# A hybrid attention layer with an MLP: the down weights of the MLP split in two by converting and adding DMAs, up and down weights in separate rings

## The chip, the cores and the metric

The kernel is one program on one core of a Trainium2 chip. The metric is device microseconds of one execution. The kernel before takes 668.31 us, the median of three runs (668.25 to 668.99).

## The reference

One decoder layer for 512 tokens of width 1024, in float32. What matters here:

```python
h = h + hybrid_mixer(rmsnorm(h, g_attn), ...)      # attention: 8 FoX heads, 8 NSA heads, one output projection
h = h + squared_relu_mlp(rmsnorm(h, g_mlp), w_up, w_down)
return rmsnorm(h, g_final)

def squared_relu_mlp(h, w_up, w_down):             # w_up 1024 x 4096, w_down 4096 x 1024
    return jnp.square(jax.nn.relu(h @ w_up)) @ w_down
```

## The kernel before

**Two halves for every operand.** TensorE reads operands rounded to a shorter float ("fp32r" in the profile). To keep float32's precision each operand is held as a rounded high part and a rounded low part (value minus high part), and each product is three matmuls into the same bank: high by high, low by high, high by low (`mm3`, lines 190 to 192). All weights lie in DRAM as one tensor `wp` of numbered pieces, each 128 partitions by 1024 (512 KB); `next_piece` counts them up, so pieces are used in a fixed order.

**Rings.** A `Ring` turns a piece into its two parts: SP loads it into a raw buffer (L139), ScalarE copies it, rounded, into the high part (L164), and a subtraction, on VectorE nearly always, gives the low part (L118). The first ring, `ring`, lies in a pool at the right end of SBUF, cuts each piece into two halves of 512 columns, and holds three pieces and two raws. When attention's first buffers are closed, a second ring, `ring2`, opens at the left end of SBUF (L1098 to L1101); it takes whole pieces, 1024 wide, and holds six and three raws. In the MLP, `mlp_piece` (L1103) takes a piece from `ring` where its number modulo 9 is below 3, and from `ring2` else. So both kinds of weights come from both rings.

**The MLP** (L1127 and on) has 8 steps. In the first half of a step, four "up" units: each multiplies one up piece with the activations `uh` and `ul` (24 matmuls of 512 columns into one bank), and ScalarE, GpSimd and VectorE turn the bank into one of four columns of `ah` and `al`: ReLU into `mt` (L1139), its square rounded into `ah` (L1140), the same square in full on GpSimd into `ma` (L1141), and `ma` less `ah` into `al` (L1142). In the second half, "down": four down pieces times `ah` and `al`, for four blocks of 128 tokens (4 times 24 matmuls), with the sums added to the residual by VectorE (L1156). The first three up units are begun inside attention's output projection, with pieces 38 to 40 from `ring`. `uh` and `ul` lie at the right end of SBUF; `ah`, `al`, `mt` and `ma` lie in the pool `mp` at the left end. In the profile's names a matmul `O<-uh,wh` belongs to an up unit (weights held in the array, activations moving), and `O<-wh,ah` to down (activations held, weights moving).

**What sets the order.** TensorE's order is the order of the code (`manual_schedule`, L75). VectorE, ScalarE, GpSimd and SP are under a second such block through the attention (L77 to L1037), so that its instructions keep the code's order among themselves; what the code has behind it a scheduler places, and it can put such an instruction between those of the attention where its buffers allow it. Each engine then runs its own list strictly in order, and so do the queues of the engines that issue DMAs.

**The end of attention**, where the MLP's first weights are prepared. Around 264 to 290 us the last attention heads are finished while NSA's half of the output projection fills TensorE. GpSimd normalises the scores `sp` (L726) and sums squares `sq` (L783). ScalarE copies the transposed scores out of the banks (`pth`, L748), copies head outputs (`ot`, L766) and scales them (`yTf`, L779); VectorE makes the low parts (`ptl` L118, `yTf` L784) and evacuates the projection's only bank "acc" into `xr` (L895), which TensorE needs empty before it begins the next unit.

Of the kernel before, what the change touches and what calls it, by code (L numbers as in the profile page):

```python
# [11 lines left out]
F32R = mybir.dt.float32r  # L12
AF = mybir.ActivationFunctionType
ALU = mybir.AluOpType

P = 128
# [37 lines left out]
def hybrid_layer(tc, x, xT, wp, wfg, cst, gfin, out):  # L54
    nc = tc.nc
    uid = [0]

    def nm(s):
        uid[0] += 1
        return f"{s}_{uid[0]}"  # L60

    def f32(ap):
        return ap.bitcast(F32)
# [3 lines left out]
    def open_pool(name, side, **kw):  # L67
        stacks[name] = ExitStack()
        return stacks[name].enter_context(tc.tile_pool(name=name, bufs=1, side=side, reuse_waits="tile", **kw))
# [37 lines left out]
    def w2k(n, dt=F32):  # L107
        return atp.tile([P, S], dt, tag="w2", name=nm(n), bufs=4)
# [4 lines left out]
    def bank(tag):  # L113
        return psp.tile([P, 512], F32, tag=tag, name=nm(tag), bufs=n_banks[tag])
# [5 lines left out]
    next_piece = [0]  # L120
# [61 lines left out]
    ring = Ring(rp, 3, 2, 2)  # L182

    def part(w, a, n):

        k, c = divmod(a, 1024 // len(w[0]))
        return w[0][k][:, c:c + n], w[1][k][:, c:c + n]

    def mm3(ps, lh, ll, rh, rl, first, last):
        nc.tensor.matmul(ps, lh, rh, start=first, stop=False)  # L190
        nc.tensor.matmul(ps, ll, rh, start=False, stop=False)  # L191
        nc.tensor.matmul(ps, lh, rl, start=False, stop=last)  # L192
# [19 lines left out]
    ps = bank("acc")  # L212
# [301 lines left out]
    w = ring.piece()  # L514
    natural_piece(q_banks, w, 3, (0,))
    ps = bank("acc")
# [34 lines left out]
    ps = bank("acc")  # L551
# [6 lines left out]
    ps = bank("T")  # L558
# [11 lines left out]
    t = w2k("f2c")  # L570
# [12 lines left out]
    for m in range(4):  # L583
        w = ring.piece()
# [44 lines left out]
    w = ring.piece()  # L629
# [3 lines left out]
    w = ring.piece()  # L633
# [240 lines left out]
    def tokens(tb):  # L874
        return slice(tb * P, tb * P + P)
# [194 lines left out]
    def up_mm(ps, w, kts):  # L1070
        for kt in kts:
            mm3(ps, *part(w, kt * P, P), uh[:, kt, :], ul[:, kt, :], kt == 0, kt == 7)
# [4 lines left out]
    for tb in range(NT):  # L1077
        ps = bank("OOSS"[tb])
# [10 lines left out]
    for i, t in enumerate(("acc", "S", "O")):  # L1089
        w = ring.piece()  # L1090
        ps = bank(t)
# [6 lines left out]

    r2p = open_pool("ring2", "left")
    mp = open_pool("mp", "left")  # L1100
    ring2 = Ring(r2p, 6, 3, 1)  # L1101

    def mlp_piece():  # L1103
        return (ring if next_piece[0] % 9 < 3 else ring2).piece()

    ssum = cp.tile([P, NT], F32, name="ssum")
    nc.vector.tensor_tensor(ssum, ssh[:, :, 0], ssh[:, :, 1], op=ALU.add)
# [8 lines left out]
    def scalar(n):  # L1116
        return cp.tile([P, 1], F32, tag="sc" + n, name=nm(n), bufs=2)
# [5 lines left out]
    def nbank():  # L1123
        un[0] += 1
        return bank(tags[un[0] % 8])

    for e in range(8):  # L1127
        ah = mp.tile([P, 4, S], F32R, tag="ah", name=nm("ah"), bufs=2)
        al = mp.tile([P, 4, S], F32R, tag="al", name=nm("al"), bufs=2)
        for f in range(4):  # L1130
            if early:
                w, ps = early.pop(0)
                up_mm(ps, w, range(4, NK))
            else:
                w, ps = mlp_piece(), nbank()
                up_mm(ps, w, range(NK))
            t = mp.tile([P, S], F32, tag="mt", name=nm("mt"), bufs=2)
            a = mp.tile([P, S], F32, tag="ma", name=nm("ma"), bufs=2)
            nc.scalar.activation(t, ps, AF.Relu)  # L1139
            nc.scalar.activation(ah[:, f, :], t, AF.Square)  # L1140
            nc.gpsimd.tensor_tensor(a, t, t, op=ALU.mult)  # L1141
            nc.vector.tensor_sub(al[:, f, :], a, f32(ah[:, f, :]))  # L1142
        wd = [mlp_piece() for _ in range(4)]
        for tb in range(NT):
            groups = [(0, 512), (512, 256), (768, 256)] if (e, tb) == (7, NT - 1) else [(0, 512), (512, 512)]
            pss = [nbank()[:, 0:n] for _, n in groups]
            tok = tokens(tb)
            for fs in ((0, 1, 2), (3,)) if tb == 0 else ((0, 1, 2, 3),):
                for ps, (c, n) in zip(pss, groups):
                    for f in fs:  # L1150
                        mm3(ps, ah[:, f, tok], al[:, f, tok], *part(wd[f], c, n), f == 0, f == 3)
            last = groups[-1]
            ob = mp.tile([P, D], F32, tag="ob", name=nm("ob"), bufs=2) if e == 7 else None
            for i, (ps, (c, n)) in enumerate(zip(pss, groups)):
                h = h1[:, tb, c:c + n]
                nc.vector.scalar_tensor_tensor(h, ps, r2s[:, tb:tb + 1], h, op0=ALU.mult, op1=ALU.add)  # L1156
                if e == 7:
                    (nc.gpsimd if i == 0 else nc.vector).tensor_tensor(ob[:, c:c + n], h, gfb[:, c:c + n], op=ALU.mult)
                    jo = mp.tile([P, S], F32, tag="mt", name=nm("jo"), bufs=2)
                    ss = sso[:, tb, i:i + 1]  # L1160
                    nc.scalar.activation(jo[:, 0:n], h, AF.Square, accum_out=ss)
                    if i == 0:
                        eb = scalar("eb")
                        nc.vector.tensor_scalar(eb, ss, 1.0 / D, EPS, op0=ALU.mult, op1=ALU.add)
                    elif i < len(groups) - 1:
                        nc.vector.scalar_tensor_tensor(eb, ss, 1.0 / D, eb, op0=ALU.mult, op1=ALU.add)
            if e == 7:
                v, t, r = scalar("v"), scalar("t"), scalar("r")
                nc.scalar.activation(t, ss, AF.Ln, scale=1.0 / D, bias=eb)
                nc.scalar.activation(r, t, AF.Exp, scale=-0.5)  # L1170
                nc.vector.scalar_tensor_tensor(v, ss, 1.0 / D, eb, op0=ALU.mult, op1=ALU.add)
                nc.vector.scalar_tensor_tensor(t, r, v, r, op0=ALU.mult, op1=ALU.mult)
                nc.vector.tensor_scalar(t, t, -0.5, 1.5, op0=ALU.mult, op1=ALU.add)
                for half in range(2):
                    cols = slice(512 * half, 512 * half + 512)
                    nc.vector.tensor_scalar(ob[:, cols], ob[:, cols], r, t, op0=ALU.mult, op1=ALU.mult)
                    nc.sync.dma_start(out[tokens(tb), cols], ob[:, cols])
# [103 lines left out]
```

## Time and profile before

| what | value |
|---|---|
| median of 3 runs | 668.31 us |
| the profiled execution's own time | 669.01 us |
| its span in the trace | 667.2 us |
| TensorE busy | 650.7 us, 98% of the span |
| VectorE, ScalarE, GpSimd busy | 405.6, 312.8, 170.6 us |
| TensorE's granted clock | full speed throughout |
| the chain that ended last | TensorE 86%, VectorE 8%, the rest 6% |
| DRAM read, mean rate | 59.81 MB, 93 GB/s over the span |

The span is the time from the first to the last instruction that the trace shows; 1.8 us of the execution lie around it. The share of TensorE says that nothing else bounds the kernel for long, and the chain agrees; the other engines have room on the whole. Between about 262 and 654 us, which holds the end of attention, the output projection and all of the MLP, TensorE shows no idle time of note.

### The profile page before, as it was taken

Reading aid. Unit: us, or ns where it says so; the run is one execution under the profiler, and the core shown is the slowest. Engines: PE = TensorE matmul, PEld = TensorE weight load, DVE = VectorE, ACT = ScalarE, POOL = GpSimd, SP = SyncE. Lnnn points to the kernel's source line nnn. Section 1 sums busy time; section 2 is a strip of 40 time slices with the busy share of each in tenths; the row PEclk is TensorE's granted clock in tenths of the full one; section 3 lists DMA queues with packets and bytes.
Section 4 is the critical chain, followed back from the end, with each engine's and each line's share of the span. In section 5 each row is a group of like instructions: output and inputs, shape, how many; then the busy total and the mean of one; then the engine's idle time right before and its main releaser. Section 6 shows DMA issues by size and latency. Waiting matters only on the chain.

```text
span 667.2 us, 9167 instructions
## 1 busy us (share of the span) xinstructions
PE 650.7 (98%) x3165; PEld 535.6 (80%) x3165; DVE 405.6 (61%) x872; ACT 312.8 (47%) x673; POOL 170.6 (26%) x203
## 2 busy tenths in 40 slices
PE   9998999999999999999999999999999999999995
PEld 7767888878787878888888888888888888888884
DVE  4798887868866789847936344354344433544146
ACT  5435536777867878637704223143142340422222
POOL 0262062655756745200301101001011020010121
PEclk9999999999999999999999999999999999999999
DMA  7723610000022573225814214143051330401002
GB/s 273 232 96 127 213 71 33 2 33 32 32 88 65 146 219 88 71 88 168 292 45 164 90 58 157 38 150 104 1 190 63 107 114 32 158 1 32 0 33 94
DMA packets 22878, 66.72 MB, mean 100 GB/s; under 512 B 4272, under 2 KB 4912, under 8 KB 22832
## 3 DMA queue, kind: packets, MB, share of 16 engines
q1 hardware_dynamic: 22688, 66.10, 29.4%
q8 instruction: 25, 0.41, 0.2%
q14 instruction: 21, 0.17, 0.1%
q10 hardware_dynamic: 144, 0.04, 0.0%
HBM read 59.81 MB, written 2.10 MB: 93 GB/s over the span
## 4 chain that ended last, share of the span: by engine, by line
PE 86%; DVE 8%; issue 2%; DMA 2%; ACT 1%; SPq 0%; POOL 0%; DVEq 0%; ACTq 0%
PE S L192 8%; PE S L190 8%; PE S L191 8%; PE acc L190 6%; PE acc L192 6%; PE acc L191 6%; PE O L190 5%; PE O L192 5%; PE O L191 5%; PE T L190 5%; PE T L192 5%; PE T L191 5%; PE O L756 4%; PE T L738 4%; PE S L710 2%
## 5 line engine op out<-in xcount | busy, mean ns | idle before, releaser
L164 ACT ACTIVATE wh<-wr 128x512 fp32r<-128x512 f32 (+1 forms) x144 | 103.5, 743 | 157.6 <-PE O L191 59.0
L118 DVE TENSOR_TENSOR wl<-wr,wh 128x512 fp32r<-128x512 f32 (+1 forms) x126 | 119.9, 971 | 93.5 <-ACT wh L164 91.6
L1141 POOL TENSOR_TENSOR ma<-mt 128x512 f32<-128x512 f32 x32 | 35.7, 1115 | 326.7 <-ACT mt L1139 326.7
L720 ACT ACTIVATE sp<-sp,st 128x128 f32<-128x128 f32 (+1 forms) x96 | 53.2, 555 | 16.9 <-DVE st L718 16.4
L718 DVE CUSTOM_DVE_ANT_0 sp<-S,c 128x128 f32<-128x128 f32 (+1 forms) x96 | 43.0, 485 | 18.7 <-PE S L711 18.2
L726 POOL TENSOR_SCALAR sp<-sp,st,gt 128x128 f32<-128x128 f32 (+1 forms) x64 | 38.5, 614 | 47.0 <-ACT sp L720 26.7
L118 DVE TENSOR_TENSOR ptl<-T,pth 128x128 fp32r<-128x128 f32 (+1 forms) x96 | 44.3, 483 | 2.9 <-ACT pth L748 2.5
L748 ACT ACTIVATE pth<-T 128x128 fp32r<-128x128 f32 (+1 forms) x96 | 38.5, 426 | 9.8 <-PE T L738 9.2
L738 PE MATMUL T<-c,sp 128*128 128x128 f32 x240 | 38.4, 273 | 3.1 <-DVE st L724 1.9
L738 PEld LDWEIGHTS T<-c,sp 128*128 128x128 f32 x240 | 29.6, 140 | 13.1 <-issue 5.1
L190 PE MATMUL S<-wh,ah 128*128 128x512 f32 (+1 forms) x100 | 38.9, 389 | 0.0
L192 PE MATMUL S<-wl,ah 128*128 128x512 f32 (+1 forms) x100 | 38.7, 387 | 0.0
L191 PE MATMUL S<-wh,al 128*128 128x512 f32 (+1 forms) x100 | 38.6, 386 | 0.0
L1156 DVE SCALAR_TENSOR_TENSOR h<-S,r2s,h 128x512 f32<-128x512 f32 (+1 forms) x25 | 18.5, 740 | 32.7 <-PE S L192 32.7
L190 PE MATMUL S<-uh,wh 128*128 128x512 f32 x88 | 34.6, 394 | 0.0
L192 PE MATMUL S<-ul,wh 128*128 128x512 f32 x88 | 34.4, 391 | 0.0
L191 PE MATMUL S<-uh,wl 128*128 128x512 f32 x88 | 34.2, 389 | 0.0
L1142 DVE TENSOR_TENSOR al<-ma,ah 128x512 fp32r<-128x512 f32 x32 | 21.8, 682 | 19.4 <-POOL ma L1141 19.4
L190 PE MATMUL acc<-xh,wh 128*128 128x512 f32 x72 | 30.9, 430 | 0.0
L192 PE MATMUL acc<-xl,wh 128*128 128x512 f32 x72 | 28.5, 395 | 0.0
L191 PE MATMUL acc<-xh,wl 128*128 128x512 f32 x72 | 28.4, 395 | 0.0
L190 PE MATMUL O<-uh,wh 128*128 128x512 f32 x72 | 28.4, 394 | 0.0
(349 smaller groups left out, 1690.3 us busy)
## 6 DMA issues: line engine op xcount, KB each, us to landing
wr<-wp_d SPq DMA_DIRECT2D x91, 512.0 KB, 3.7
wx<-wp_d SPq DMA_DIRECT2D x10, 512.0 KB, 4.2
xr<-x_d SPq DMA_DIRECT2D x4, 512.0 KB, 7.3
out_d<-ob SPq DMA_DIRECT2D x8, 256.0 KB, 2.1
xr<-xT_d SPq DMA_DIRECT2D x3, 512.0 KB, 6.6
fq<-tqh SPq DMA_DIRECT2D x8, 128.0 KB, 4.0
fq<-tq SPq DMA_DIRECT2D x8, 128.0 KB, 3.4
f2q<-tqh SPq DMA_DIRECT2D x8, 128.0 KB, 3.1
```

What stands on the lines that cost most here:

```text
L118: eng.tensor_tensor(o, a, b, op=ALU.subtract)
L164: high = lambda: nc.scalar.activation(hi, raw[:, c], AF.Copy)
L190: nc.tensor.matmul(ps, lh, rh, start=first, stop=False)
L191: nc.tensor.matmul(ps, ll, rh, start=False, stop=False)
L192: nc.tensor.matmul(ps, lh, rl, start=False, stop=last)
L718: nc.vector.tensor_tensor_reduce(out=self.p[i], in0=self.ps[i], in1=self.bias(i), scale=1.0, scalar=1e35, op0=ALU.add, op1=ALU.min, accum_ ...
L720: nc.scalar.activation(self.p[i], self.p[i], AF.Exp, bias=m, scale=-1.0, accum_out=den)
L726: nc.gpsimd.tensor_scalar(self.p[i], self.p[i], rs, g, op0=ALU.mult, op1=ALU.mult)
L738: nc.tensor.transpose(pt[:, j * P:j * P + P], self.p[i][:, j * P:j * P + P], ident)
L748: nc.scalar.activation(self.blocks(self.th, i), self.pt[i], AF.Copy)
L756: nc.tensor.matmul(o[:, j * P:S], self.v(j), t[:, 4 * j * P:(3 * j + NT) * P], start=first and part == 0 and j == 0, stop=last and part == ...
L1141: nc.gpsimd.tensor_tensor(a, t, t, op=ALU.mult)
```

## The change

Down weights no longer go through a ring. A function `down_piece` takes the next piece and makes its two parts with two DMAs that GpSimd issues and one copy of ScalarE: a DMA that converts while it moves writes the rounded high part `dh` (L1109 of the kernel after); ScalarE writes the negative of it into `dl` (L1110); and a second DMA reads the same piece again and adds it to `dl` (L1111), rounded. There are 32 such pieces, so 64 DMAs of 512 KB. Raw buffers, SP's loads, ScalarE's high copies (L164) and VectorE's low subtractions (L118) of the down pieces go. The buffers for `dh` and `dl` (six each, 1024 wide) stand where the parts of `ring2` stood. All up weights now come from `ring`. And the square of the up units is made once, by ScalarE, into `ma`, then copied, rounded, into `ah`; GpSimd's square is gone.

```diff
     r2p = open_pool("ring2", "left")
     mp = open_pool("mp", "left")
-    ring2 = Ring(r2p, 6, 3, 1)
-
-    def mlp_piece():
-        return (ring if next_piece[0] % 9 < 3 else ring2).piece()
+    ring.auto = 0
+
+    def down_piece():
+
+        i = next_piece[0]
+        next_piece[0] += 1
+        hi = r2p.tile([P, 1024], F32R, tag="wh", name=nm("dh"), bufs=6)
+        lo = r2p.tile([P, 1024], F32R, tag="wl", name=nm("dl"), bufs=6)
+        nc.gpsimd.dma_start(hi, wp[i])
+        nc.scalar.activation(lo, f32(hi), AF.Copy, scale=-1.0)
+        nc.gpsimd.dma_start(lo, wp[i], accum_op=ALU.add)
+        return [hi], [lo]
...
-                w, ps = mlp_piece(), nbank()
+                w, ps = ring.piece(), nbank()
...
             nc.scalar.activation(t, ps, AF.Relu)
-            nc.scalar.activation(ah[:, f, :], t, AF.Square)
-            nc.gpsimd.tensor_tensor(a, t, t, op=ALU.mult)
+            nc.scalar.activation(a, t, AF.Square)
+            nc.scalar.activation(ah[:, f, :], a, AF.Copy)
             nc.vector.tensor_sub(al[:, f, :], a, f32(ah[:, f, :]))
-        wd = [mlp_piece() for _ in range(4)]
+        wd = [down_piece() for _ in range(4)]
```

The line `ring.auto = 0` sets what was already so. TensorE's list keeps its order. The lists of the other engines change, and not only in the MLP: since the six buffers of `dh` and `dl` are free once attention's first pools are closed, the scheduler puts the first six down pieces among the last attention heads.

GpSimd's list at the end of attention (`sp` is the normalising, `sq` the sum of squares; `dh` and `dl` are the new DMAs):

```order
 L783 TENSOR_TENSOR sq_3294<-sq_3294,sq_3098 128x512
+L1109 DMA dh_3934<-wp_d 128x1024
 L726 TENSOR_SCALAR sp_3268<-sp_3268,st_3269 128x512
 L726 TENSOR_SCALAR sp_3324<-sp_3324,st_3325 128x128
 L726 TENSOR_SCALAR sp_3328<-sp_3328,st_3329 128x256
 L726 TENSOR_SCALAR sp_3335<-sp_3335,st_3336 128x384
+L1109 DMA dh_3939<-wp_d 128x1024
+L1109 DMA dh_3944<-wp_d 128x1024
+L1111 DMA dl_3935<-wp_d 128x1024
 L726 TENSOR_SCALAR sp_3361<-sp_3361,st_3362 128x512
+L1111 DMA dl_3940<-wp_d 128x1024
 L783 TENSOR_TENSOR sq_3445<-sq_3445,sq_3294 128x512
```

Five DMAs have come between GpSimd's normalisings: one behind `sq_3294`, three behind the run of four `sp`, one before the next `sq`.

ScalarE's list at the same place (`pth` copies transposed scores, `yTf` is a head's scaled output, and each `dl` copy waits until the DMA of the `dh` that it reads has landed):

```order
 L164 ACTIVATE wh_3354<-wr_3017 128x512
+L1110 ACTIVATE dl_3935<-dh_3934 128x1024
 L748 ACTIVATE pth_3342<-T_3398 128x4x128
 L766 ACTIVATE ot_3412<-O_3383 64x512
 L748 ACTIVATE pth_3417<-T_3419 128x128
 L748 ACTIVATE pth_3417<-T_3419 128x2x128
+L1110 ACTIVATE dl_3940<-dh_3939 128x1024
 L748 ACTIVATE pth_3417<-T_3434 128x3x128
 L778 ACTIVATE sq_3445<-oo_3381 128x512
 L779 ACTIVATE yTf_2800<-oo_3381,c_98 128x512
+L1110 ACTIVATE dl_3945<-dh_3944 128x1024
 L748 ACTIVATE pth_3417<-T_3458 128x4x128
```

Three copies of down weights now stand in front of three copies of transposed scores.

ScalarE's list some ten microseconds on, at the last head pair (`wh` here is an output projection weight, `ot` and `yTf` the last head's):

```order
+L1110 ACTIVATE dl_3950<-dh_3949 128x1024
 L164 ACTIVATE wh_3587<-wr_3585 128x512
+L1110 ACTIVATE dl_4233<-dh_4232 128x1024
 L766 ACTIVATE ot_3532<-O_3517 64x512
+L1110 ACTIVATE dl_4238<-dh_4237 128x1024
 L778 ACTIVATE sq_3535<-oo_3471 128x512
 L779 ACTIVATE yTf_2800<-oo_3471,c_98 128x512
```

The other three of the first six copies stand between the instructions that finish the last head pair.

## Rows read from the trace of the kernel before

**Rows 1.** Busy time of each engine over the whole span (first part of the page)

```profile
PE 650.7 (98%) x3165; PEld 535.6 (80%) x3165; DVE 405.6 (61%) x872; ACT 312.8 (47%) x673; POOL 170.6 (26%) x203
```

**Rows 2.** Windows, one stretch inside the MLP: busy time by engine, clock, DMA

```profile
core 0: us, PE busy (x) PEld busy (x) DVE busy (x) ACT busy (x) POOL busy (x), PEclk, DMA share, GB/s
340.00:380.00 40.00, 40.00 (x176) 32.85 (x175) 17.64 (x22) 12.78 (x19) 4.17 (x4) 1.00 0.30 105
```

**Rows 3.** Timeline of TensorE: first matmul of half steps (start, duration, instruction)

```profile
330.13 0.39 PE L190 MATMUL T<-wh,ah 128*128 128x512 f32 x1
352.26 0.39 PE L190 MATMUL T<-uh,wh 128*128 128x512 f32 x1
374.14 0.39 PE L190 MATMUL S<-wh,ah 128*128 128x512 f32 x1
395.91 0.39 PE L190 MATMUL S<-uh,wh 128*128 128x512 f32 x1
...
505.06 0.39 PE L190 MATMUL T<-wh,ah 128*128 128x512 f32 x1
527.25 0.40 PE L190 MATMUL T<-uh,wh 128*128 128x512 f32 x1
549.19 0.39 PE L190 MATMUL S<-wh,ah 128*128 128x512 f32 x1
571.36 0.40 PE L190 MATMUL S<-uh,wh 128*128 128x512 f32 x1
593.34 0.39 PE L190 MATMUL T<-wh,ah 128*128 128x512 f32 x1
615.55 0.40 PE L190 MATMUL T<-uh,wh 128*128 128x512 f32 x1
```

**Rows 4.** Timeline of GpSimd at the end of attention

```profile
264.95 1.29 POOL L783 TENSOR_TENSOR sq<-sq,sq 128x512 f32<-128x512 f32 x1 [0.65 <-ACT sq L778]
268.67 2.07 POOL L726 TENSOR_SCALAR sp<-sp,st 128x512 f32<-128x512 f32 x4 [2.42 <-DVE st L724]
```

**Rows 5.** Timeline of ScalarE at the end of attention

```profile
270.23 1.13 ACT L164 ACTIVATE wh<-wr 128x512 fp32r<-128x512 f32 x2
...
274.41 0.49 ACT L748 ACTIVATE pth<-T 128x384 fp32r<-128x384 f32 x1 [1.00 <-PE T L738]
...
286.87 0.71 ACT L779 ACTIVATE yTf<-oo,c 128x512 fp32r<-128x512 f32 x1
```

**Rows 6.** Timeline of VectorE at the end of attention

```profile
275.04 0.56 DVE L118 TENSOR_TENSOR ptl<-T,pth 128x384 fp32r<-128x384 f32 x1
276.44 0.75 DVE L895 SCALAR_TENSOR_TENSOR xr<-acc,rn,xr 128x512 f32<-128x512 f32 x1 [0.84 <-PE acc L192]
...
287.62 0.75 DVE L784 SCALAR_TENSOR_TENSOR yTf<-oo,c,yTf 128x512 fp32r<-128x512 f32 x1
```

**Rows 7.** Timeline of TensorE at the end of attention

```profile
277.26 0.49 PE L190 MATMUL acc<-wh,yTn 128*128 128x512 f32 x1
...
289.62 0.39 PE L190 MATMUL S<-wh,yTf 128*128 128x512 f32 x1
```

**Rows 8.** DMA issues (last part of the page): count, size, median us to landing

```profile
wr<-wp_d SPq DMA_DIRECT2D x91, 512.0 KB, 3.7
...
xr<-x_d SPq DMA_DIRECT2D x4, 512.0 KB, 7.3
```

**Rows 9.** Timeline of SP's queue: one DMA issue

```profile
308.32 0.33 SPq L1112 DMA_DIRECT2D gfb<-gfin_d  x1
```

**Rows 10.** Timeline of all engines, last up unit of a step

```profile
418.03 0.60 ACT L1139 ACTIVATE mt<-O 128x512 f32<-128x512 f32 x1 [3.86 <-PE O L192]
418.52 1.05 ACT L164 ACTIVATE wh<-wr 128x1024 fp32r<-128x1024 f32 x1
418.70 1.04 POOL L1141 TENSOR_TENSOR ma<-mt 128x512 f32<-128x512 f32 x1 [4.45 <-ACT mt L1139]
419.47 0.62 ACT L1140 ACTIVATE ah<-mt 128x512 fp32r<-128x512 f32 x1
419.60 1.22 DVE L118 TENSOR_TENSOR wl<-wr,wh 128x1024 fp32r<-128x1024 f32 x1 [4.20 <-ACT wh L164]
420.75 0.68 DVE L1142 TENSOR_TENSOR al<-ma,ah 128x512 fp32r<-128x512 f32 x1
```

## The prediction

> **What bounds the kernel now.** I read the busy times first: TensorE has 650.7 of 667.2 us, and VectorE, ScalarE and GpSimd 405.6, 312.8 and 170.6 [rows 1]. The reader is to see that work which the change takes from the other engines buys nothing by itself. The window inside the MLP says it sharper: 40.00 of 40.00 us on TensorE at full clock, ScalarE 12.78, GpSimd 4.17, DMA busy at 0.30 of its engines' time while it moves 105 GB/s [rows 2]. So the change can act in two ways only: through the pace of the matmuls themselves, or through a wait that TensorE doesn't have now.
>
> For the pace I took the times at which half steps begin [rows 3]. Each half has 96 matmuls, and they don't all take equally long. Down of step 1 runs from 374.14 to 395.91, 21.77 us, or 226.8 ns a matmul. Down of step 0 takes 352.26 − 330.13 = 22.13, of step 4 22.19, of step 5 22.17, of step 6 22.21. By the rule `i % 9 < 3` the down weights of steps 1, 2 and 3 come from `ring2` alone, those of the others have one to three pieces from `ring`. Up halves show it in smaller steps: 21.88 in step 1 (two pieces from `ring2`), 21.94 in step 5 (three), 21.98 in step 6 (four), against 21.77 for a clean half: 0.055, 0.057 and 0.053 us a piece. In every slow stretch weights lie at the end of SBUF opposite to what they are multiplied with (`uh` and `ul` right, `ah` and `al` left); in every clean one all of it lies at one end. TensorE has no gap in either, so nothing is waited for; the matmuls start 2% further apart.
>
> For waits I read the end of attention engine by engine [rows 4 to 7], then DMA landings [rows 8] and issue [rows 9], and the last up unit of a step [rows 10].
>
> **The change part by part. Pace.** After it all up weights lie right, with `uh`, and all down weights left, with `ah`. Each half should take the clean 21.77. Down: 0.36 (step 0) + 0.42 + 0.40 + 0.44 (steps 4 to 6) + 0.44 (step 7, taken as step 6) = 2.06 us. Up: the rule gives 18 pieces from `ring2` (1, 2, 1, 1, 2, 3, 4, 4 in the eight steps; pieces 38 to 40 are fetched early from `ring`) at 0.054 = 0.97. Gain 3.03 us. The ends: 0, if the place isn't the cause, and 3.03; I take 3.03, since every half measured falls in line.
>
> The Trainium skill would speak against that term. "SBUF — State Buffer", section "Who interferes with whom", gives TensorE read ports of its own and lets only the pair of VectorE and GpSimd contend; by it the place of an operand costs nothing, the gain is 0, and the time is that of the fourth rival below. The 22.13 to 22.21 against 21.77 of rows 3 differ without a wait in sight, so I follow the rows; that place, and not something that goes with it, makes the difference no row shows.
>
> **Work that goes or moves in the MLP.** VectorE loses 32 subtractions (1.22 us each [rows 10]), SP 32 loads, GpSimd 32 squares (1.04). ScalarE swaps 32 high copies of 1.05 for 32 negative copies of the same shape, and gets 32 more copies of about 0.62. It is busy 12.78 of 40 us [rows 2], so all this counts 0. The chain behind the last up unit: now `mt` begins at 418.03 and `al` ends at 421.43. After: 0.60 + 0.62 + 0.62 + 0.68 with the same handovers end no later than that, as VectorE no longer has a 1.22 us subtraction in the way. TensorE wants it after 18 matmuls of the down half, 395.91 + 21.77 + 4.08 = 421.76. Cost 0; if a 1.05 us copy stood in front of `mt`, it would be late by about 1.
>
> **The 64 DMAs in the steady state.** They add 16.8 MB, 2.1 MB in a step of 43.5 us. At 105 GB/s for a share of 0.30 [rows 2] a full set of engines moves 350 GB/s, so 512 KB take 1.5 us and the eight DMAs of a step 12. GpSimd issues four converting and two adding DMAs from the freeing of the first buffer (2 us before a down half ends) to the last piece that the next one needs (25.9 us after, by the 21.77 + 4.08 above). With c for a converting and 2c for an adding DMA, which reads its target too, 8c must fit into some 25 us: c up to 3.1 us, twice the plain rate's. I take it as fitting, cost 0. The other end: c = 4 is 7 us short in each of seven steps, +49 us.
>
> **The six early pieces.** Here the change adds waits on the path. Let L be the time from GpSimd's turn to issue a converting DMA until it has landed. The first, behind `sq` at 266.24, falls into GpSimd's idle 2.42 us [rows 4]. The second waits until the four `sp` end at 270.74. Its negative copy stands in front of the `pth` copy of 274.41 [rows 5], behind which `ptl` (0.56) and the `xr` evacuation at 276.44 stand on VectorE [rows 6], and that frees the only "acc" bank for the matmul at 277.26 [rows 7]. So: landing 270.74 + L, plus 1.05 copy, 0.49 `pth`, 0.56 `ptl`, 0.75 `xr`, and 0.2 of handovers, is when TensorE goes on. The three later copies delay the last `yTf` (286.87), VectorE's low part of it (287.62) and the matmuls of 289.62 in the same way: the third copy must be done before GpSimd passes its adding DMA and issues the next three, so that a second L is in series.
>
> L isn't in the trace, for GpSimd issues no DMA. Nearest rows: 3.7 us for SP's loads of this size, 7.3 for the slowest ones [rows 8]. I take 3.7 plus a GpSimd instruction (1.04, [rows 10]) in place of SP's issue (0.33, [rows 9]): 4.4. Then TensorE goes on at 270.74 + 4.4 + 3.05 = 278.2 in place of 277.26, +0.95. For `yTf`: the copy of the third piece ends at 279.05; GpSimd issues its adding DMA and three converting ones until 283.2; these land at 284.6, 285.6 and 286.6; with the copies between them `yTf`'s low part ends at 291.1, where TensorE, 0.95 late, would want it at 290.8: +0.3. Sum 1.25. At L = 3.7 it is about 0; with two L's in series a further microsecond of L costs about 2, so 7.3 costs some 7.
>
> By the Trainium skill, "DMA: Bandwidth & Descriptors", section "Anatomy of one DMA — SWDGE (gpsimd) path", a DMA of GpSimd takes 2.0 us plus its bytes at 436 GB/s, an estimate of 3.2 us here; by that the boundary would cost nothing and the time would be about 665.3. No row shows such a DMA, and a plain load of SP takes 3.7.
>
> **Sum.** On the profiled execution 669.01 (span 667.2 and 1.8 around it): −3.03 + 1.25 = −1.78, 667.2. That execution lies 0.70 above the median of the runs, 668.31, so the forecast there is 666.5.
>
> **The rivals.** A measurement tells 0.2%, 1.34 us, from no change.
>
> First: L is 4.6 to 6 us, since the converting DMAs share one queue with adding ones that read twice as much. For it: the order puts an adding DMA between them. Against: in the second piece's case only converting ones are ahead. At 5.2: 668.31 − 3.03 + 1.25 + 1.6 = 668.1, no change.
>
> Second, slower: L as in the slowest loads. For it: 7.3 is a row. Against: those loads are issued four together. 668.31 − 3.03 + 7 = 672.3; it decides from a cost of 4.4, L about 6.
>
> Third, slower: adding DMAs run so slowly that c passes 3.1 and the down weights come late in every step. 690 (c = 3.5) to 715. For it: nothing in the trace is of this kind; against: twice the plain time is allowed for. The Trainium skill has a rule for it: "Collectives: The Full Stack", Part 3, says that an adding transfer needs two source reads and halves the rate; that much has a place in the 2c.
>
> Fourth, the change doesn't do what it says: the pace stays, the boundary costs its 1.25: 669.6. For it: the place is only inferred. Against: the halves fall in line.
>
> **How the numbers follow.** The forecast has 0.42, the first rival 0.25, the second 0.13, the third 0.10, the fourth 0.10. Faster by over 0.2% is the forecast, 0.42; within it the first rival and half of the fourth, 0.30; slower the rest, 0.28. The forecast's own range is 665.2 (whole pace, L at 3.7) to 667.0. The range for 8 in 10 reaches over the first, the fourth and nearly all of the second: 665.1 to 673.0.
>
> **What would show it.** Right: all half steps take 21.77; the first converting DMAs land in about 4.4; the matmul after `xr` begins about 1 us later against its predecessors. Wrong: halves of 21.9 and 22.2 remain; idle TensorE at the beginning of a down half, with "DMA" or ScalarE's `dl` as releaser; idle time of several microseconds around 277 or 289; or GpSimd's list behind its issues, with `sp` late.

## The result and the profile after

The kernel after takes 675.34 us, the median of four runs (674.91 to 675.68), beside 668.65 for the kernel before on the same chip: a ratio of 1.0094, with an interval of 1.0074 to 1.0115. It is slower by 0.94%, some 6.3 us, where 1.8 us of gain were forecast, and it lies outside the range of 665.1 to 673.0. The span of the profiled execution is 673.1 us, 5.9 more than before.

Two parts of the page after, the busy times and the DMA issues (count, size, median us from issue to landing):

```profile
PE 651.1 (97%) x3165; PEld 537.3 (80%) x3165; DVE 366.9 (55%) x848; ACT 330.7 (49%) x713; POOL 180.7 (27%) x235
...
wr<-wp_d SPq DMA_DIRECT2D x59, 512.0 KB, 4.0
dh<-wp_d POOLq DMA_DIRECT2D x32, 512.0 KB, 5.3
dl<-wp_d POOLq DMA_DIRECT2D x32, 512.0 KB, 8.7
```

VectorE lost 39 us of work against [rows 1], and the time didn't fall for it. The new DMAs land in 5.3 and 8.7 us in the middle, where SP's loads take 4.0.

**The gain came as forecast.** The timeline of TensorE after, the same half steps as in [rows 3]:

```profile
338.65 0.39 PE L190 MATMUL T<-dh,ah 128*128 128x512 f32 x1
360.42 0.39 PE L190 MATMUL T<-uh,wh 128*128 128x512 f32 x1
382.22 0.39 PE L190 MATMUL S<-dh,ah 128*128 128x512 f32 x1
404.00 0.39 PE L190 MATMUL S<-uh,wh 128*128 128x512 f32 x1
...
512.98 0.39 PE L190 MATMUL T<-dh,ah 128*128 128x512 f32 x1
534.75 0.39 PE L190 MATMUL T<-uh,wh 128*128 128x512 f32 x1
...
600.13 0.39 PE L190 MATMUL T<-dh,ah 128*128 128x512 f32 x1
621.90 0.39 PE L190 MATMUL T<-uh,wh 128*128 128x512 f32 x1
```

The down halves shown take 21.77 or 21.78 (360.42 − 338.65, 404.00 − 382.22, 534.75 − 512.98, 621.90 − 600.13), and no down half takes more than 21.81; every whole up half takes 21.80 or 21.81 (382.22 − 360.42 = 21.80). Before, they took up to 22.21 and 21.98. But the first down half begins at 338.65, and in [rows 3] at 330.13: 8.52 us late. The last matmul of the MLP starts at 665.51 against 659.76, 5.75 late. So the MLP gave back 2.77 us, and 8.5 had been lost ahead of it.

**The loss.** The waits of TensorE between 262 and 300 us (total, times, longest):

```profile
PE S L190 <- ACT yTf L779: 4.1, 1, 4.1
PE acc L190 <- DVE xr L895: 1.2, 1, 1.2
```

No such row is there before. Windows of the same stretch, the kernel before first (columns as in [rows 2]):

```profile
270.00:280.00 10.00, 10.00 (x55) 8.30 (x54) 8.86 (x17) 7.84 (x15) 2.71 (x4) 1.00 0.14 54
280.00:290.00 10.00, 10.00 (x48) 8.32 (x47) 5.45 (x9) 4.00 (x8) 0.00 (x0) 1.00 0.34 107
290.00:300.00 10.00, 10.00 (x50) 8.35 (x49) 4.64 (x11) 2.90 (x9) 0.00 (x0) 1.00 0.30 104
```

and after:

```profile
270.00:280.00 10.00, 10.00 (x55) 8.27 (x54) 8.88 (x16) 9.43 (x19) 7.37 (x11) 1.00 0.77 211
280.00:290.00 10.00, 8.80 (x42) 7.25 (x41) 3.29 (x6) 1.55 (x3) 1.08 (x2) 1.00 1.06 304
290.00:300.00 10.00, 5.91 (x17) 4.03 (x16) 3.94 (x6) 6.24 (x9) 2.63 (x3) 0.69 0.90 192
```

The last column but one is the lesson: the share of the DMA engines went from 0.14 and 0.34 to 0.77 and 1.06, which is full (above 1, the times of packets overlap), and ScalarE did only 1.55 us of work in ten. In the third window the granted clock is 0.69. What ScalarE stood at, from its timeline after:

```profile
274.73 1.06 ACT L1110 ACTIVATE dl<-dh 128x1024 fp32r<-128x1024 f32 x1 [0.49 <-DMA dh<-wp_d]
...
281.66 1.16 ACT L164 ACTIVATE wh<-wr 128x512 fp32r<-128x512 f32 x2 [1.27 <-DMA wr<-wp_d]
290.08 1.06 ACT L1110 ACTIVATE dl<-dh 128x1024 fp32r<-128x1024 f32 x1 [7.26 <-DMA dh<-wp_d]
...
294.77 0.71 ACT L779 ACTIVATE yTf<-oo,c 128x512 fp32r<-128x512 f32 x1
```

and GpSimd's issues (duration of the issue, and of several in a row):

```profile
270.94 1.13 POOL L1109 DMA_DIRECT2D dh<-wp_d  x2
272.86 0.91 POOL L1111 DMA_DIRECT2D dl<-wp_d  x1 [0.79 <-ACT dl L1110]
...
276.09 0.91 POOL L1111 DMA_DIRECT2D dl<-wp_d  x1 [1.20 <-ACT dl L1110]
...
278.54 0.89 POOL L1111 DMA_DIRECT2D dl<-wp_d  x1 [0.20 <-DMA wr<-wp_d]
279.12 1.96 POOL L1109 DMA_DIRECT2D dh<-wp_d  x3
```

The second converting DMA, issued at 270.94, was there by 274.73: 3.8 us, better than the 4.4 of the forecast. The fourth, issued at 279.12, was there at 290.08: 11 us. Between the two stand three adding DMAs, of 272.86, 276.09 and 278.54. The copy of the fourth piece kept ScalarE waiting for 7.26 us, with `yTf` behind it, 294.77 in place of 286.87 in [rows 5]. The chain of the trace goes through the fifth, which landed just behind the fourth (start, length, what):

```profile
278.54 0.89 POOL dl L1111
...
279.67 12.18 DMA dh<-wp_d
...
292.83 0.58 ACT ot L766
293.40 0.80 ACT dl L1110
...
294.87 0.62 ACT yTf L779
```

The smaller wait, 1.2 us, shows up in another queue: SP's load of an output projection weight came late, so ScalarE's `wh` at 281.66 waited 1.27 us for it, VectorE's `wl` waited for that, and the evacuation behind it was late for TensorE. SP's loads between 262 and 300 us, before (count, size, median us to landing):

```profile
wr<-wp_d SPq DMA_DIRECT2D x5, 512.0 KB, 3.2
```

and after:

```profile
wr<-wp_d SPq DMA_DIRECT2D x4, 512.0 KB, 7.3
```

VectorE's timeline after:

```profile
282.33 1.29 DVE L118 TENSOR_TENSOR wl<-wr,wh 128x512 fp32r<-128x512 f32 x2 [1.00 <-ACT wh L164]
283.54 0.75 DVE L895 SCALAR_TENSOR_TENSOR xr<-acc,rn,xr 128x512 f32<-128x512 f32 x1
```

**The clock.** TensorE behind the 4.09 us of idle time:

```profile
291.04 0.40 PE L192 MATMUL acc<-wl,yTf 128*128 128x512 f32 x1
295.54 0.80 PE L190 MATMUL S<-wh,yTf 128*128 128x512 f32 x1 [4.09 <-ACT yTf L779]
...
299.90 0.63 PE L190 MATMUL acc<-wh,yTf 128*128 128x512 f32 x1
300.33 0.57 PE L191 MATMUL acc<-wh,yTf 128*128 128x512 f32 x1
300.74 0.40 PE L192 MATMUL acc<-wl,yTf 128*128 128x512 f32 x1
```

Eleven matmuls start in the 5.20 us from 295.54 to 300.74, most of them 0.427 us apart, where 0.229 is the pace at the full clock: the granted clock had fallen to its lower level, 1.2 GHz, while TensorE was idle. In narrower windows it is 1.00 up to 293.40 and 0.50 from 294.40 to 300.00. 5.20 − 11 × 0.229 = 2.68 us.

The account of the 8.52: 1.20 and 4.09 idle, 2.68 of clock, 0.24 by which this execution was late already at 262 us, and 0.31 that I don't place.

### The profile page after: what moved, and what is told of

Read it like the earlier page. It is cut to its first block, busy times and chain, and to the rows that moved or that the text cites. A ratio compares the mean times of both kernels' runs of the same rounds, so it can differ in the third digit from the quotient of the medians.

```text
span 673.1 us, 9116 instructions
## 1 busy us (share of the span) xinstructions
PE 651.1 (97%) x3165; PEld 537.3 (80%) x3165; DVE 366.9 (55%) x848; ACT 330.7 (49%) x713; POOL 180.7 (27%) x235
## 4 chain that ended last, share of the span: by engine, by line
PE 81%; DVE 8%; DMA 5%; issue 2%; ACT 2%; SPq 0%; POOL 0%; DVEq 0%; ACTq 0%
PE S L192 8%; PE S L190 7%; PE S L191 7%; PE acc L190 5%; PE acc L192 5%; PE acc L191 5%; PE O L190 5%; PE O L192 5%; PE O L191 5%; PE T L192 5%; PE T L190 5%; PE T L191 5%; PE T L738 4%; PE O L756 4%; PE S L710 2%
## 5 line engine op out<-in xcount | busy, mean ns | idle before, releaser
L118 DVE TENSOR_TENSOR wl<-wr,wh 128x512 fp32r<-128x512 f32 x102 | 76.1, 759 | 112.2 <-ACT wh L164 111.9
L1110 ACT ACTIVATE dl<-dh 128x1024 fp32r<-128x1024 f32 x32 | 33.7, 1057 | 174.6 <-DMA dh<-wp_d 174.5
L164 ACT ACTIVATE wh<-wr 128x512 fp32r<-128x512 f32 x120 | 72.1, 622 | 40.1 <-DMA wr<-wp_d 28.0
L1109 POOL DMA_DIRECT2D dh<-wp_d x32 | 20.0, 647 | 235.5 <-PE O L192 233.9
L720 ACT ACTIVATE sp<-sp,st 128x128 f32<-128x128 f32 (+1 forms) x96 | 53.2, 556 | 17.1 <-DVE st L718 16.5
L1111 POOL DMA_DIRECT2D dl<-wp_d x32 | 28.3, 883 | 73.5 <-ACT dl L1110 72.7
L118 DVE TENSOR_TENSOR ptl<-T,pth 128x128 fp32r<-128x128 f32 (+1 forms) x96 | 44.3, 482 | 3.6 <-ACT pth L748 3.3
L191 PE MATMUL S<-dh,al 128*128 128x512 f32 (+1 forms) x100 | 38.5, 385 | 0.0
L192 PE MATMUL S<-dl,ah 128*128 128x512 f32 (+1 forms) x100 | 38.5, 385 | 0.0
L190 PE MATMUL S<-dh,ah 128*128 128x512 f32 (+1 forms) x100 | 38.5, 385 | 0.0
L1150 DVE TENSOR_TENSOR al<-ma,ah 128x512 fp32r<-128x512 f32 x32 | 22.2, 693 | 28.1 <-ACT ah L1149 28.1
```

The lines of the kernel that those rows point to most:

```text
L118: eng.tensor_tensor(o, a, b, op=ALU.subtract)
L164: high = lambda: nc.scalar.activation(hi, raw[:, c], AF.Copy)
L720: nc.scalar.activation(self.p[i], self.p[i], AF.Exp, bias=m, scale=-1.0, accum_out=den)
L1110: nc.scalar.activation(lo, f32(hi), AF.Copy, scale=-1.0)
L1111: nc.gpsimd.dma_start(lo, wp[i], accum_op=ALU.add)
```

## The experiments

Two questions: does the even pace come from the place of the operands, and what exactly made the loss? Ratios stand against the kernel before, run on the same chip. There it took 669.1 to 671.2 us in the middle, and the expected times were made for 668.3, so they are compared by ratio times 668.3.

**place**: the kernel before with sorted rings (all up weights from `ring`, all down weights from `ring2`), and nothing else of the change.

```diff
-                w, ps = mlp_piece(), nbank()
+                w, ps = ring.piece(), nbank()
...
-        wd = [mlp_piece() for _ in range(4)]
+        wd = [ring2.piece() for _ in range(4)]
```

> The kernel before with one edit: all up weights from the right ring, all down weights from the left one, both still loaded by SP. Theory 1 (the pace of the matmuls follows where the weights lie, and nothing else in the change touches it): all halves of steps take 21.77 to 21.81 us, time 668.3 - 3.0 = 665.3. Rival (the even pace came from the other DMAs or from the engines that now do less or more): halves of 21.9 to 22.2 remain, time 668.3.

Measured 666.65, ratio 0.9948 (0.9931 to 0.9965), which is 664.8 by ratio. From step 1 on all halves take 21.77 and 21.80. The first down half takes 22.35: VectorE's lows of later down pieces now stand in front of an `al`, and TensorE idles 0.3 us for it. So the gain needs none of the new DMAs.

**mp_below** and **mp_right**: which property of the place? In every slow half before, two things go together: the operands lie at opposite ends, and the one held in the array lies at the lower address. From place, the pool of `ah` and `al` is put below the down weights, or at the other end:

```diff
-    r2p = open_pool("ring2", "left")
     mp = open_pool("mp", "left")
+    r2p = open_pool("ring2", "left")
...
-    mp = open_pool("mp", "left")
+    mp = open_pool("mp", "right")
```

(the first three lines are mp_below, the last two mp_right)

> The kernel with SP's loads and sorted rings (run place), but the pool of ah and al opened before the left ring, so that these lie below the down weights and not above them; all still at the left end. Theory 1a (opposite ends of SBUF make the matmuls slower): down halves stay at 21.77, time as place, 666.6. Rival 1b (it is slow where the operand held in the array lies at a lower address than the one that moves, as in every slow half before): all eight down halves take about 22.2, time 666.6 + 8 x 0.43 = 670.1.

> As place, but the pool of ah and al opened at the right end, the down weights still at the left end. Theory 1a (opposite ends): all eight down halves take about 22.2, time 670.1. Rival 1b (order of the two addresses): held operand above the moving one, so down halves stay at 21.77, time 666.6.

A down half and the up half behind it, TensorE's timeline of mp_below:

```profile
373.25 0.39 PE L190 MATMUL S<-wh,ah 128*128 128x512 f32 x1
395.02 0.39 PE L190 MATMUL S<-uh,wh 128*128 128x512 f32 x1
```

and of mp_right:

```profile
373.67 0.39 PE L190 MATMUL S<-wh,ah 128*128 128x512 f32 x1
396.07 0.39 PE L190 MATMUL S<-uh,wh 128*128 128x512 f32 x1
```

21.77 and 22.40, and so in all steps; the programs of TensorE are the same. Times: 666.19 (0.9960, 0.9938 to 0.9981) and 672.20 (1.0045, 1.0022 to 1.0069). Opposite ends cost, the order of the addresses doesn't: rival 1b falls. The price is larger than 22.2 would have it, 0.63 us a half or 6.6 ns a matmul, and the time by ratio, 671.3, is longer too. This is shown for the down halves. For the up halves, where a far piece costs some 0.05 us, only place speaks: sorted, they are even, but `ring` and `ring2` also differ in the width of their buffers, and no run takes the two apart.

**early_off**: all six early pieces wait for `rf`, which VectorE has only when attention is over.

```diff
+        if i < 52:
+            nc.vector.tensor_copy(hi[:, 0:1], rf[:, 0:1])
         nc.gpsimd.dma_start(hi, wp[i])
```

> The kernel after, but the converting DMAs of the first pieces wait for a number that is ready only when attention is over (a one-column copy from rf by VectorE). Theory 2 (the whole loss is made by the early pieces at the end of attention: idle TensorE of 1.2 and 4.1 us, and the low clock behind it): no idle time at 280 to 296, clock stays at 1.00, time 665.3 to 666. Rival (adding DMAs cost time in the steps of the MLP too, hidden behind the late start): 667 or more, with idle TensorE inside the MLP.

Measured 675.76, 1.0083 (1.0063 to 1.0104). Theory 2 falls in the form it had, and the rival is nearer, though only the entry of the MLP and its step 0 idle and no step behind them. The stretch at 280 to 296 is clean, but the crowd has only moved. ScalarE's waits between 300 and 345 us:

```profile
ACT dl L1112 <- DMA dh<-wp_d: 10.6, 2, 5.9
ACT wh L164 <- DMA wr<-wp_d: 3.2, 1, 3.2
```

Now the copies stand in front of `uh` and `ah`, the DMA engines are full from 310 to 330 (1.05 and 1.07), and TensorE idles 2.3 us for `ul` and 2.0 for `ah`, each time with a lower clock after it. So it isn't the end of attention that makes the loss, but several converting and adding DMAs at once in front of work that ScalarE does in order.

**adds_later** and **copies_later** take this apart: in the first only the adding DMAs wait for `rf`, in the second the copies too.

```diff
         nc.scalar.activation(lo, f32(hi), AF.Copy, scale=-1.0)
+        if i < 52:
+            nc.vector.scalar_tensor_tensor(lo[:, 0:1], rf[:, 0:1], 0.0, f32(lo[:, 0:1]), op0=ALU.mult, op1=ALU.add)
         nc.gpsimd.dma_start(lo, wp[i], accum_op=ALU.add)
...
+        if i < 52:
+            nc.vector.tensor_copy(lo[:, 0:1], rf[:, 0:1])
         nc.gpsimd.dma_start(hi, wp[i])
```

> The kernel after, but only the adding DMAs of the first pieces wait for rf; converting DMAs and ScalarE's copies stay early. Theory 2a (the engines are full: adding DMAs take some 3 us of all 16 engines, converting ones 1.3, and the late converting DMAs stand behind three adding ones): the fourth to sixth converting DMAs land in 4 to 6 us, not 9 to 10, idle TensorE at the yTf wait falls from 4.1 to below 1.5, time 666 to 668. Rival 2b (any copy of ScalarE that waits for a DMA of GpSimd in that place costs as much): 672 or more.

> The kernel after, but ScalarE's negative copies of the first pieces, and so the adding DMAs, wait for rf; only converting DMAs stay early. Theory 2: nothing on ScalarE waits for a DMA of GpSimd before the MLP, no idle TensorE at 280 to 296, 665.3 to 666. Rival 2c (the early DMAs hurt by taking the engines from SP's loads of output projection weights): idle TensorE of 1 us or more stays, 667 or more.

adds_later: 672.46, 1.0039 (1.0024 to 1.0053). The reading at the place asked for is clear: the six early converting DMAs land in 4.6 us in the middle, where in the kernel after they took 7.7, and TensorE has no wait left between 263 and 300 us, though all copies of ScalarE are where they were. Rival 2b falls. The time, 670.9 by ratio, is longer than expected by a thing not counted: six adding DMAs now start together at 303, and SP's loads of up weights run into them. DMA issues between 302 and 325 us, and ScalarE's waits from 300 to 345:

```profile
dl<-wp_d POOLq DMA_DIRECT2D x6, 512.0 KB, 12.7
wr<-wp_d SPq DMA_DIRECT2D x3, 512.0 KB, 9.0
```

```profile
ACT wh L164 <- DMA wr<-wp_d: 9.1, 2, 5.3
```

SP's loads take 9.0, where in the same stretch of the kernel before eleven of them took 5.3 in the middle. They are in another queue than the adding DMAs, and the share of the DMA engines is 1.05 between 310 and 320, so I take it that it is the engines that are shared, not the queue alone. TensorE idles 3.8 us for it.

copies_later: 666.60, 0.9959 (0.9944 to 0.9973), with no wait of TensorE behind 263 us and all halves even. Here each adding DMA follows its copy, and ScalarE spreads them over 309 to 319 us. By ratio that is 665.6, as theory 2 has it; rival 2c falls. The DMA engines are as full here (1.02 and 1.05 in the two windows from 310 to 330), and SP's loads take 7.6 between 302 and 325: full engines cost nothing where nothing that TensorE is about to need waits for them. Nor is it faster than place, so these runs show no gain from the 64 DMAs themselves.

**no_adds** prices the two kinds: no adding DMA at all (this output leaves the low part's correction out).

```diff
-        nc.gpsimd.dma_start(lo, wp[i], accum_op=ALU.add)
```

> The kernel after without the adding DMAs: the low part of the down weights is then minus the high part, so the output leaves the correction out. Theory 2a: a converting DMA takes about 1.3 us of all 16 engines and an adding one the rest, some 3.1 (64 DMAs of GpSimd took 141 us of them in the kernel after): the share of the software queue falls from 21.0% to 6 or 7%; early copies stay in ScalarE's list, but no idle TensorE over 1 us at 280 to 296; time 665.5 to 667. Rival (converting is as dear as adding): share 10.5%, and idle time of 1 us or more stays.

The software queue after (packets, MB, share of 16 engines), and in no_adds:

```profile
q0 software_dynamic: 9216, 33.56, 21.0%
```

```profile
q0 software_dynamic: 4608, 16.78, 7.7%
```

7.7% of 665.4 us over 32 DMAs is 1.60 us of all 16 engines for a converting one, as much as for a plain load (29.4% of 667.2 us for 66.10 MB in the page of before gives 1.56 for 512 KB). If the converting ones cost as much in the kernel after, the 32 adding ones have the rest of 21.0% of 673.1: (141.4 − 51.2) / 32 = 2.82, an estimate, since overlapping times of packets are counted in it. The Trainium skill ("Collectives: The Full Stack", Part 3) gives ReduceScatter, whose add needs two source reads, about half the rate of AllGather, which copies. Here the adding DMA takes 1.76 times the converting one. The time was 667.22, of a single run, and at 280 to 296 TensorE waited for nothing over 0.2 us; the first down half begins at 331.01, where it begins at 330.13 before and at 338.65 after. So early converting DMAs and copies alone cost little.

**adds_first3** and **adds_last3**: which of the adding DMAs? Only the first three wait for `rf`, or only the last three (the condition of adds_later is `i < 45`, or `45 <= i < 52`).

> As adds_later, but only the first three adding DMAs (pieces 42 to 44) wait for rf; the fourth to sixth are issued as soon as their copies are done, behind all six converting DMAs. Theory 2a (the three adding DMAs ahead of the fourth converting one make the loss, some 2.8 us of all engines each): no idle TensorE at the yTf wait, and three adding DMAs at once behind rf hold SP's up weights up half as long as six did: time 666.5 to 669. Rival 2d (any three early adding DMAs do it, wherever they stand): idle time of 3 us or more at 285 to 296, time 672 or more.

> The reverse: the first three adding DMAs stay early as in the kernel after, the last three wait for rf. Theory 2a: the fourth converting DMA lands 9 to 11 us after its issue as in the kernel after, idle time before yTf 3.5 to 4.5 us and low clock behind it; time about that of the kernel after, 673 to 676. Rival 2d: the loss is halved, 670 to 671.

TensorE's waits between 262 and 650 us in adds_first3:

```profile
PE T L1065 <- DVE ul L1067: 2.6, 1, 2.6
PE S L191 <- DVE yTf L784: 0.3, 1, 0.3
```

and in adds_last3:

```profile
PE S L190 <- ACT yTf L779: 4.3, 1, 4.3
PE T L1065 <- DVE ul L1067: 2.8, 1, 2.8
PE acc L190 <- DVE xr L895: 1.1, 1, 1.1
```

With the first three out of the way the wait for `yTf` is down to 0.3; with only them early it is as large as in the kernel after. Rival 2d falls at that place. What no run takes apart is how the three hold the fourth converting DMA up: by standing ahead of it in GpSimd's queue, or by filling the engines. Both kernels have a second wait at the entry of the MLP, of three adding DMAs in a burst. The times are 671.49 (1.0007, 0.9988 to 1.0026) and 679.75 (1.0135, 1.0104 to 1.0165). By ratio that is 668.8, inside what was expected, and 677.3, 1.3 above it: in the second I had left the wait at the entry out.

## Why the prediction was wrong

**The pace: right.** 3.03 us were forecast; from the first down half to the end the MLP gave 2.77. The difference is that a clean up half takes 21.80, not 21.77 (seven times 0.03: no clean up half was among the rows), and that the up piece of step 0 lies ahead of that stretch (0.05). That opposite ends are the cause, which was only inferred, mp_right and mp_below showed for the down halves. The page "SBUF — State Buffer" of the Trainium skill ("Who interferes with whom") gives TensorE read ports of its own that nobody shares; mp_right, 22.40 against 21.77 with the same instructions, shows that the place of its operands matters all the same.

**Work that goes or moves, and the steady state: right.** Both were costed at 0. No half of the kernel after has a wait in the MLP, and 1.60 and 2.82 us for the two kinds of DMA are near the 1.5 of the plain rate and twice that.

**The early pieces: wrong, and it decided the sign.** The step that failed is the sentence that the fourth to sixth converting DMAs, issued until 283.2, "land at 284.6, 285.6 and 286.6". It used one L of 4.4 for all of them, and so had `yTf` late by 0.3 us; TensorE waited 4.09 for it and then ran 2.68 us at the lower clock. L was near enough for the second (3.8): its term of 0.95 came to nothing, the matmul of 277.26 begins at 277.51 in an execution 0.24 late already, and nothing waited for the first and the third. The 1.20 us by way of SP's late load had no term at all. L isn't a property of the DMA but of what is under way: the fourth took 11 us with three adding DMAs ahead of it. The numbers for this stood in the prediction already: five converting DMAs behind the first at 1.5 and three adding ones at 3 make 16.5 us of all engines, and they were given the 15.7 us from 270.9 to 286.6, in which SP's loads take their part too. The sum was made for a step of the MLP, where the window showed a share of 0.30, and not for the stretch where the scheduler had put the first six.

The first rival named this mechanism, that converting DMAs share a queue with adding ones, and priced it with an L of 5.2, at 668.1. Against it I wrote that for the second piece only converting ones are ahead; that was true, and the second piece wasn't the one that mattered. The second rival, L as in the slowest loads, came nearest (672.3, with 7 us lost at the end of attention, where 8.5 were), but from loads of another queue and kind. Neither had the clock: 2.68 us of the loss came after the wait, and TensorE doesn't idle for so long in the kernel before, so that no row of it has that price.

## What to carry to other kernels

Before asking how long a DMA takes, add up what all 16 engines have to move in the stretch where it will be issued; the sum belongs there and not to the steady state. A wait that stands in an in-order list in front of the critical engine's supply costs its length, and a few microseconds more if TensorE falls idle and comes back at the lower clock. The gain here needed a few lines: operands that meet in a matmul at one end of SBUF (place, mp_below), or the new DMAs with copies that come only when attention is over (copies_later), all faster than both kernels, at 0.995 to 0.996 of the kernel before, which these runs don't tell apart.

## What was not expected

One down piece of four at the other end already slows the whole half: 22.13 and 22.19 with one, 22.17 with two, 22.21 with three, 22.40 with four. (The 22.40 is of mp_right, where the activations lie at the other end and the weights stay.) So it isn't only the matmuls that read the far piece: in step 0 of the kernel before, those of the three near pieces start 231.7, 229.2 and 231.7 ns apart in the mean, those of the far one 229.6, where 226.8 is the clean pace. Why, the runs don't show.
